# Five small reorderings in a decoder step on one core: a query broadcast moved to another queue, weight splits ahead of key pages, two groups of stores and sums put elsewhere

## The chip, the cores and the metric

The kernel runs on one core of a Trainium2 chip. The metric is the device time of one execution in microseconds (us). Three runs of the kernel before took 1029.35, 1026.24 and 1020.0 us, so the median is 1026.24 us. A core has four compute engines that run their own instruction streams in order: TensorE (PE, matrix products), VectorE (DVE), ScalarE (ACT) and GpSimd (POOL). SyncE (SP) only starts transfers here. ACT and POOL start transfers too.

## What is computed

The reference is one layer of a hybrid decoder for 512 prompt tokens and 8 sample tokens that share all weights (520 columns in all, called NT in the code; they are worked in two halves of 260).

```python
h = rms_norm(x, norm1_g) * (1.0 + sc1) + sh1
z = h @ w_in                       # xr, gr, q, k, v, forget logits, ga, gb
xc, conv_new = causal_dwconv(xr, conv_buf, conv_w, conv_b)
hr, h_last = rg_lru(xc, h0, pos0, rg_wr, rg_br, rg_wi, rg_bi, rg_lambda)
ya = (hr * jax.nn.gelu(gr)) @ w_proj_a
yb = attend(q, k, v, logf).reshape(B, T, ATTN_W) @ w_proj_b   # samples: paged cache of 1024 rows
mixed = (jax.nn.sigmoid(ga) * ya + jax.nn.sigmoid(gb) * yb) @ w_o
x = x + g1 * mixed
h2 = rms_norm(x, norm2_g) * (1.0 + sc2) + sh2
gu, up = jnp.split(h2 @ w_ffn_in, 2, axis=-1)
x = x + g2 * ((jax.nn.silu(gu) * up) @ w_ffn_out)
```

The outputs are the final norm of x, the new keys, values and forget values, the last three inputs of the convolution (convT) and the last state of the recurrence (rgT).

## The kernel before, in words

**Products.** Everything is held transposed, features on the 128 partitions and tokens along the row. Every float32 operand of a large product is split into a high and a low part (for weights `whi` and `wlo`, for h `hh` and `hl`), and a product of one 128-feature weight tile by eight k tiles is 24 matmuls of 260 columns for each half: high by high, low by high, high by low. A weight travels in *chunks* of 256 columns from memory into `wraw` (SP, L210; two buffers), ACT casts the high part (L246), DVE subtracts it to get the low part (L248). A *unit* is one such 128-column weight tile; units are numbered by `state["n"]` in the order in which PE uses them. Unit 0 and 1 are the query tiles q6 and q7, units 2 and 3 are the convolution inputs xr0 and xr1 (one chunk, one `wraw`), unit 4 is the gate tile ga0. `begin()` (L285) opens a unit: it runs `tick()`, then loads chunks ahead, then splits weights ahead (`split_upto`), then issues stores. The list of instructions in each engine is laid down by a scheduler from the order of the code, from dependencies and from explicit ties (`issue_after`), so an edit in the code need not move anything.

**Queries.** The tiles q0 to q5 are made from two partial sums: PE makes the second half and DVE adds the first (L926). `q_done` (L878) stores the query tile, and transposes its sample columns on PE into `qt` (L883), from which the samples' queries go through memory (`qtd`) and come back spread over all partitions as `qb`. `after[0] = after[1]` (L928) ties the low parts of units 0 and 1 behind the add of query tile 2.

**Keys of the cache.** `tick()` multiplies key pages of the samples by the broadcast query (L743, `pg<-pg,qb`) and sums them by head (L744), on DVE. `key_halves` (L707) loads two half pages on POOL and, for the first pages of a sample, issues the broadcast of half a query row (L716), on POOL as well. Its second broadcast (sample 1, first half) stands on POOL behind the running sums of the forget values (`after`, L456).

**Decays.** `decay_load` (L1211) reads rows of forget sums spread over the partitions (`fb<-ftd`, L1214) on SP, for attention over the prompt. The stores of convT and rgT (L1136, L1137) stand ahead of it in the code.

**Join.** The samples' attention over the cache ends in `fold_values` (L849: one product `pvs` on PE, one copy `pvt` on ACT), and `join_values` (L1351) mixes it with the new token's value on DVE (L1355 to L1357) and writes it into the sample columns of the operand of w_proj_b (L1359 on ACT, L1360 on DVE). `join()` runs both in the middle of the first half of the first w_proj_b product, and the second half of that product reads the result. On POOL, L1306 finishes the prompt part of the last tile of that operand.

**Norm 2 and block sums.** `h2_half(1)` (L1484) makes the second half of h2 tile by tile f = 0 to 7: DVE scales x (L1500), POOL finishes the sample columns (L1502, L1503), ACT casts the high part (L1505, L1511), DVE (even f) or ACT (odd f) finishes the float32 value (L1509, L1507), DVE subtracts to get the low part (L1512). PE consumes tile after tile in the first products of the feed-forward layer (L305 `fi`). The rest of that layer uses sums of blocks of h2: `h2_blocks(k)` (L1631) makes four differences on POOL from tiles k and k + 4, for k = 0 to 3, and DVE and ACT split them later (`split_blocks`, L1640).

## Time and profile before

| | us |
|---|---|
| runs shown | 1029.35, 1026.24, 1020.0 (median 1026.24) |
| the profiled execution | 1021.18 |
| its span, first to last instruction | 1019.1 |
| outside the span (1021.18 - 1019.1) | 2.1 |
| PE busy | 994.4 |
| DVE busy | 793.0 |
| ACT busy | 548.2 |
| POOL busy | 329.4 |

The page gives the granted clock of PE as 0.997 of full speed over the span. The timeline view has one row for an instruction or a run of equal ones: its start and its duration in us from the start of the span, engine, source line, operation, the written tile `<-` the read ones, the count after an x, and in brackets the idle time ahead of it with what ended it. PE's matmuls overlap: a row lasts some 0.28 us, but the next one starts 0.12 us after it, so time lost on PE is read from the starts of two rows: their distance less 0.12. SPq is the queue of transfers that SP starts; a DMA row there is the issue, not the transfer. The waits view adds up such idle times by waiting and releasing instruction.

### The profile page before, as it was taken

The numbers are of one execution on the slowest core, as the hardware profiler recorded it, in microseconds if no ns is written. First come the engines' busy times: TensorE is split into PE (matmuls) and PEld (weight loads), VectorE is DVE, ScalarE is ACT, GpSimd is POOL, SyncE is SP. The second block draws the span as 40 slices with busy tenths as digits, with TensorE's granted clock in tenths as the row PEclk, the third lists the DMA queues.
The fourth block names the chain that finished last, engine by engine and source line by source line (L and its number), as shares of the span: only waits on it lengthen the run. The fifth ranks groups of instructions, "written<-read, shape, count | busy, mean of one in ns | idle before, by whom it ended". The sixth has DMA issues, their size and how long they took to land.

```text
span 1019.1 us, 21277 instructions
## 1 busy us (share of the span) xinstructions
PE 994.4 (98%) x8012; PEld 920.4 (90%) x8012; DVE 793.0 (78%) x1423; ACT 548.2 (54%) x1128; POOL 329.4 (32%) x416
## 2 busy tenths in 40 slices
PE   5999999999999999999999999999999999999996
PEld 2799999999998988888888888999999999999996
DVE  5559999998998887887655544868888888888865
ACT  4534476858761576777783233554444444445453
POOL 0347211111134146554500001583342433425112
PEclk9999999999999999999999999999999999999998
DMA  9797857788889999997867996324234243233222
GB/s 325 250 326 261 253 184 196 231 269 271 283 260 331 342 301 280 309 275 242 254 212 265 319 329 196 83 64 125 80 107 123 65 125 87 81 104 104 63 64 84
DMA packets 164313, 206.97 MB, mean 203 GB/s; under 512 B 9826, under 2 KB 125042, under 8 KB 164146
## 3 DMA queue, kind: packets, MB, share of 16 engines
q1 hardware_dynamic: 147490, 152.52, 48.2%
q0 software_dynamic: 13040, 46.67, 13.9%
q10 hardware_dynamic: 3680, 6.42, 1.7%
q8 instruction: 63, 1.03, 0.4%
q14 instruction: 40, 0.33, 0.1%
HBM read 192.49 MB, written 13.09 MB: 202 GB/s over the span
## 4 chain that ended last, share of the span: by engine, by line
PE 89%; DMA 4%; DVE 2%; ACT 1%; issue 1%; POOL 1%; POOLq 0%; SPq 0%; DVEq 0%; ACTq 0%
PE fo L305 12%; PE k L305 5%; PE wo L305 5%; PE gb L305 5%; PE gr L305 5%; PE ga L305 5%; PE pb L305 5%; PE v L305 4%; PE xr L305 4%; PE pv L836 3%; PE pa L305 3%; PE po L1301 2%; PE qp L540 2%; PE ada L372 2%; PE ptt L1267 2%; PE fi L305 1%
## 5 line engine op out<-in xcount | busy, mean ns | idle before, releaser
L246 ACT CAST whi<-wraw 128x1024 fp32r<-128x1024 f32 (+1 forms) x79 | 82.0, 1039 | 110.7 <-PE pb L305 34.3
L248 DVE TENSOR_TENSOR wlo<-wraw,whi 128x1024 fp32r<-128x1024 f32 (+1 forms) x79 | 99.2, 1256 | 21.2 <-ACT whi L246 18.8
L270 ACT CAST wb<-ws 128x512 fp32r<-128x512 f32 x72 | 44.8, 622 | 93.2 <-PE fo L305 64.6
L305 PE MATMUL fo<-ach,wb 128*128 128x260 f32 x512 | 93.5, 282 | 0.0
L698 POOL DMA_DIRECT2D pg<-in_cache_k_dram x74 | 39.6, 536 | 144.9 <-DVE S L748 62.8
L271 DVE TENSOR_TENSOR wb<-wraw,wb 128x512 fp32r<-128x512 f32 x86 | 75.6, 879 | 5.9 <-ACT wb L270 4.7
L305 PEld LDWEIGHTS fo<-ach,wb 128*128 128x128 f32 x512 | 79.1, 188 | 0.0
L271 DVE TENSOR_TENSOR wb<-ws,wb 128x512 fp32r<-128x512 f32 x72 | 64.4, 894 | 14.1 <-ACT wb L270 12.2
L261 POOL TENSOR_TENSOR ws<-wraw 128x512 f32<-128x512 f32 x18 | 24.5, 1361 | 156.9 <-DMA wraw<-in_w_fi_dram 92.0
L305 PE MATMUL fo<-acl,wb 128*128 128x260 f32 x256 | 72.5, 283 | 0.0
L270 ACT CAST wb<-wraw 128x512 fp32r<-128x512 f32 x86 | 53.5, 622 | 33.3 <-ACT cp L1676 6.4
L747 DVE TENSOR_TENSOR pg<-pg,qb 128x1024 f32<-128x1024 f32 x48 | 57.8, 1218 | 3.0 <-DMA pg<-in_cache_k_dram 3.0
L748 DVE TENSOR_REDUCE S<-pg 128x16 f32<-128x1024 f32 x48 | 57.4, 1208 | 0.2
L1258 POOL TENSOR_SCALAR p<-p,mu 128x128 f32<-128x128 f32 (+3 forms) x28 | 38.6, 1391 | 53.1 <-DVE mu L1254 47.2
L305 PEld LDWEIGHTS fo<-acl,wb 128*128 128x128 f32 x256 | 48.1, 188 | 0.0
L1252 ACT ACTIVATE p<-p,mu 128x128 f32<-128x128 f32 (+3 forms) x64 | 35.4, 554 | 18.0 <-DVE mu L1251 17.8
L305 PE MATMUL v<-hh,whi 128*128 128x260 f32 x128 | 37.3, 292 | 0.8 <-ACT row L816 0.5
L305 PE MATMUL pb<-oh,whi 128*128 128x260 f32 x128 | 37.2, 291 | 0.3 <-ACT oh L1359 0.3
L305 PE MATMUL xr<-hh,wlo 128*128 128x260 f32 x128 | 36.3, 283 | 1.1 <-DVE wlo L248 1.1
L305 PE MATMUL k<-hh,whi 128*128 128x260 f32 x128 | 37.3, 291 | 0.0
L305 PE MATMUL gb<-hh,whi 128*128 128x260 f32 x128 | 37.0, 289 | 0.0
L305 PE MATMUL xr<-hh,whi 128*128 128x260 f32 x128 | 36.7, 287 | 0.0
(1101 smaller groups left out, 3957.0 us busy)
## 6 DMA issues: line engine op xcount, KB each, us to landing
araw<-in_ada_w_dram SPq DMA_DIRECT2D x48, 512.0 KB, 7.6
wraw<-in_w_fi_dram SPq DMA_DIRECT2D x44, 512.0 KB, 4.2
pg<-in_cache_k_dram POOLq DMA_DIRECT2D x42, 512.0 KB, 6.3
pg<-in_cache_v_dram SPq DMA_DIRECT2D x42, 512.0 KB, 5.3
wraw<-in_w_in_dram SPq DMA_DIRECT2D x34, 512.0 KB, 7.9
wraw<-in_w_in_dram SPq DMA_DIRECT2D x11, 1024.0 KB, 8.9
pg<-in_cache_v_dram POOLq DMA_DIRECT2D x22, 512.0 KB, 6.4
pg<-in_cache_k_dram POOLq DMA_DIRECT2D x32, 256.0 KB, 5.2
```

The source lines that it names most:

```text
L246: state["act"] = act.copy(hi[:, :k1 - k0], src)
L248: state["last"] = dve.tensor_tensor(lo[:, :k1 - k0], src, hi[:, :k1 - k0].bitcast(F32), ALU.subtract)
L261: pool.tensor_tensor(s1, a21, a22, ALU.add)
L270: state["act"] = act.copy(t[:, :4], src)
L271: state["last"] = dve.tensor_tensor(t[:, 4:], src, t[:, :4].bitcast(F32), ALU.subtract)
L305: state["mm"] = pe.matmul(out[:, :t1 - t0], lhsT=wt[k], rhs=at, start=k == 0 and m == 0, stop=k == nk - 1 and m == 2)
L698: done.append(eng.dma_start(pg, cache[bass.ds(r, 1), :, c0:c1].rearrange("a p c -> (a p) c")))
L747: dve.tensor_tensor(pg, pg, q, ALU.mult)
L748: last = dve.tensor_reduce(S[r // 2][:, c:c + H], pg.rearrange("p (h d) -> p h d", d=DH), AX.X, ALU.add)
L836: pe.matmul(pv[0][32 * gq:32 * gq + 32, :], lhsT=pw[r][:, c:c + 32], rhs=pgs[gq // 2][:, 512 * hf:512 * hf + 512], start=j == 0, stop=j == ...
L1252: act.activation(p[:, :n + 128], p[:, :n + 128], AF.Exp, bias=mu[:, 0:1], scale=-1.0, accum_out=mu[:, 1:2])
L1258: (pool.tensor_scalar(p, p, mu[:, 2:3], None, ALU.mult) if a and i + 1 < KT else act.activation(p, p, AF.Copy, scale=mu[:, 2:3]))
```

## The change

1. *Queries.* The tie of units 0 and 1 moves from the add of query tile 2 to that of tile 3.
2. *Splits ahead of key pages.* When unit 1 opens, the weights are split ahead first, and only then `tick()` runs.
3. *A query broadcast on SP.* While `state["n"]` is 1, `key_halves` issues the query broadcast on SP instead of POOL. That is the one for sample 1, first half.
4. *Decay loads ahead of two stores.* The stores of convT and rgT stand in the code behind the first key product, the query loads and the decay loads.
5. *Join.* `fold_values` runs ahead of the first w_proj_b product instead of inside it, and the two products in `join_values` change places.
6. *Block sums.* The four groups go in the order k = 3, 0, 1, 2; the first instruction is now the one that reads the second halves of tiles 3 and 7, and all others are tied behind it.

```diff
@@ begin
+        if n == 1:
+            split_upto(reach(n, last, state["lead"]))
         if n < 42:
             tick(KEYS[n], n in VALUES)
@@ key_halves
-            pool.dma_start(qb[0], qtd[s:s + 1, 512 * half:512 * half + 512].partition_broadcast(128))
+            eng = sp if state["n"] == 1 else pool
+            eng.dma_start(qb[0], qtd[s:s + 1, 512 * half:512 * half + 512].partition_broadcast(128))
@@ queries
-                if i == 2:
+                if i == 3:
                     after[0] = after[1] = state["qadd"]
@@ behind the recurrence
-    sp.dma_start(convT, conv_out)
-    sp.dma_start(rgT, rg_out)
@@ join_values
+        dve.tensor_tensor(v8v, v8v, xv[:, :, 1], ALU.mult)
         dve.tensor_tensor(o8v, pvv, xv[:, :, 0], ALU.mult)
-        dve.tensor_tensor(v8v, v8v, xv[:, :, 1], ALU.mult)
@@ ahead of the attention
     decay_load(0)
+    sp.dma_start(convT, conv_out)
+    sp.dma_start(rgT, rg_out)
@@ last attention tile
             some_values(32)
+            assert not values_todo and not chains
+            fold_values(*pv.pop("todo"))
@@ join
-        assert not values_todo and not chains
-        fold_values(*pv.pop("todo"))
         join_values()
@@ h2_blocks
-        pool.tensor_tensor(u[:, L_], b1[:, R_], b1[:, L_], ALU.subtract)
-        pool.tensor_tensor(w[:, L_], b2[:, R_], u[:, L_], ALU.subtract)
-        pool.tensor_tensor(w[:, R_], b2[:, R_], b1[:, R_], ALU.subtract)
-        pool.tensor_tensor(u[:, R_], b2[:, L_], w[:, L_], ALU.subtract)
-        traw.append((u, w))
+        with tc.issue_after(state["blocks"].ins) if k != 3 else nullcontext():
+            first = pool.tensor_tensor(w[:, R_], b2[:, R_], b1[:, R_], ALU.subtract)
+        if k == 3:
+            state["blocks"] = first
+        with tc.issue_after(state["blocks"].ins):
+            pool.tensor_tensor(u[:, L_], b1[:, R_], b1[:, L_], ALU.subtract)
+            pool.tensor_tensor(w[:, L_], b2[:, R_], u[:, L_], ALU.subtract)
+            pool.tensor_tensor(u[:, R_], b2[:, L_], w[:, L_], ALU.subtract)
+        traw[k] = u, w
@@ feed-forward
-            for k in range(4):
+            for k in (3, 0, 1, 2):
                 h2_blocks(k)
```

The built programs show what moved. The first place is DVE while PE makes the query tiles q3 and q4 (`q3_0` is the first half of tile 3, `wlo_711` and `wlo_756` are units 0 and 1). Before:

```order
L926 TENSOR_TENSOR qp_109<-q2_1_659,qp_109 128x260
L248 TENSOR_TENSOR wlo_711<-wraw_565,whi_710 128x1024
L926 TENSOR_TENSOR qp_110<-q3_0_679,qp_110 128x260
L926 TENSOR_TENSOR qp_110<-q3_1_693,qp_110 128x260
L248 TENSOR_TENSOR wlo_756<-wraw_565,whi_755 128x1024
L926 TENSOR_TENSOR qp_111<-q4_0_723,qp_111 128x260
```

On DVE at the same place, now:

```order
L929 TENSOR_TENSOR qp_109<-q2_1_659,qp_109 128x260
L929 TENSOR_TENSOR qp_110<-q3_0_679,qp_110 128x260
L929 TENSOR_TENSOR qp_110<-q3_1_693,qp_110 128x260
L248 TENSOR_TENSOR wlo_711<-wraw_565,whi_710 128x1024
L248 TENSOR_TENSOR wlo_756<-wraw_565,whi_755 128x1024
L929 TENSOR_TENSOR qp_111<-q4_0_723,qp_111 128x260
```

Both low parts now stand behind the two adds of query tile 3; the first one stood ahead of them.

The second place is DVE ahead of xr1 (`wlo_1063` is unit 2, `wlo_1186` unit 3, `wlo_1258` unit 4, `qb_1037` the broadcast that goes to SP, `gws` splits of the recurrence's gate weights). Before:

```order
L248 TENSOR_TENSOR wlo_1063<-wraw_759,whi_1062 128x1024
L914 TENSOR_TENSOR gws_1121<-gw_917,gws_1121 128x256
L914 TENSOR_TENSOR gws_1124<-gw_917,gws_1124 128x256
L743 TENSOR_TENSOR pg_1016<-pg_1016,qb_1037 128x1024
L743 TENSOR_TENSOR pg_1039<-pg_1039,qb_1037 128x1024
L744 TENSOR_REDUCE S_761<-pg_1016 128x2x8
L744 TENSOR_REDUCE S_761<-pg_1039 128x2x8
L248 TENSOR_TENSOR wlo_1186<-wraw_759,whi_1185 128x1024
L743 TENSOR_TENSOR pg_1143<-pg_1143,qb_1037 128x1024
```

On DVE there, now (unit 3 is `wlo_1140`):

```order
L917 TENSOR_TENSOR gws_1124<-gw_917,gws_1124 128x256
L248 TENSOR_TENSOR wlo_1140<-wraw_759,whi_1139 128x1024
L746 TENSOR_TENSOR pg_1016<-pg_1016,qb_1037 128x1024
L746 TENSOR_TENSOR pg_1039<-pg_1039,qb_1037 128x1024
L747 TENSOR_REDUCE S_761<-pg_1016 128x2x8
L747 TENSOR_REDUCE S_761<-pg_1039 128x2x8
L746 TENSOR_TENSOR pg_1147<-pg_1147,qb_1037 128x1024
L746 TENSOR_TENSOR pg_1168<-pg_1168,qb_1037 128x1024
L747 TENSOR_REDUCE S_761<-pg_1147 128x2x8
L747 TENSOR_REDUCE S_761<-pg_1168 128x2x8
L248 TENSOR_TENSOR wlo_1258<-wraw_1060,whi_1257 128x1024
```

The low part of unit 3 went ahead of the first four key instructions; unit 4 still stands behind all eight. On SP the new broadcast stands between the chunk of unit 4 and the store of query tile 6, and the next chunk's load stands ahead of the store of query tile 7 instead of behind it.

The third place is POOL behind norm 2 (`h2r_9373`, `9386`, `9399`, `9412` hold tiles 0 and 1, 2 and 3, 4 and 5, 6 and 7). Before:

```order
L1503 TENSOR_TENSOR h2r_9412<-h2r_9412,mod_102 128x2x8
L1634 TENSOR_TENSOR u_9961<-h2r_9373 128x260
L1636 TENSOR_TENSOR w_9962<-h2r_9399,h2r_9373 128x260
L1635 TENSOR_TENSOR w_9962<-h2r_9399,u_9961 128x260
L1634 TENSOR_TENSOR u_9967<-h2r_9373 128x260
L1637 TENSOR_TENSOR u_9961<-h2r_9399,w_9962 128x260
```

On POOL at the same place, now (`u_9961` and `w_9962` are those of k = 3):

```order
L1506 TENSOR_TENSOR h2r_9412<-h2r_9412,mod_102 128x2x8
L1638 TENSOR_TENSOR w_9962<-h2r_9412,h2r_9386 128x260
L1642 TENSOR_TENSOR u_9961<-h2r_9386 128x260
L1638 TENSOR_TENSOR w_9968<-h2r_9399,h2r_9373 128x260
L1643 TENSOR_TENSOR w_9962<-h2r_9412,u_9961 128x260
L1642 TENSOR_TENSOR u_9967<-h2r_9373 128x260
```

The first block sum now reads tiles 3 and 7, so all sixteen stand behind the last tile of norm 2; they began with tiles 0 and 4.

Of the rest: on PE `pvs` (one product) stands directly behind `xp` and ahead of the first w_proj_b matmul, where twelve of that product's matmuls stood ahead of it. On SP the order around edit 4 is the same in both programs: the stores of rgT and convT, the loads qA and qB, then the loads `fb`. The number of matmuls, splits and transfers is the same.

More of the change, by code (lines that the diff above doesn't have):

```diff
@@ L1628 @@
     L_, R_ = slice(0, HALF), slice(HALF, NT)
-    tb, traw = [], []
+    tb, traw = [], {}
     def h2_blocks(k):
```

## The prediction

> **What bounds the kernel now.** I read the page's busy times first, then the waits of PE alone, then the timeline around each of those waits on the engines that end it.
>
> ```profile
> PE 994.4 (98%) x8012; PEld 920.4 (90%) x8012; DVE 793.0 (78%) x1423; ACT 548.2 (54%) x1128; POOL 329.4 (32%) x416
> ...
> PE fi L305 <- DVE h2l L1512: 1.1, 2, 0.8
> PE xr L305 <- DVE wlo L248: 1.1, 1, 1.1
> PE qt L883 <- DVE qp L926: 0.8, 1, 0.8
> PE pv L836 <- DMA pg<-in_cache_v_dram: 0.4, 1, 0.4
> ...
> PE pb L305 <- ACT oh L1359: 0.3, 1, 0.3
> ```
>
> PE is busy 98% of the span, and no matmul is removed, so the only thing to win is idle time of PE. The waits name five stops that the edits touch: the feed-forward start (1.1), xr1 (1.1), the query transposes (0.8), the value pages (0.4), the join (0.3), 3.7 us together. Behind each of them PE goes on without a long idle stretch, so a stop that goes moves all that follows, and the end with it. Nothing here can be worth 1% (10 us); the danger is only that something new makes PE wait.
>
> **Edit 1, query transposes.** Timeline of PE, then of DVE:
>
> ```profile
> 61.89 0.28 PE L540 MATMUL q<-hl,whi 128*128 128x260 f32 x1
> ...
> 62.48 0.29 PE L540 MATMUL q<-hh,whi 128*128 128x260 f32 x1
> 63.59 0.27 PE L883 MATMUL qt<-cs,qp 128*8 128x128 f32 x1 [0.83 <-DVE qp L926]
> ...
> 61.64 1.23 DVE L248 TENSOR_TENSOR wlo<-wraw,whi 128x1024 fp32r<-128x1024 f32 x1 [2.00 <-ACT whi L246]
> 62.78 0.76 DVE L926 TENSOR_TENSOR qp<-q,qp 128x260 f32<-128x260 f32 x2
> ```
>
> The transposes of tile 3 start 1.11 us behind the matmul ahead of them, 0.99 more than the 0.12 step. The tile's last matmul ends at 62.17, but DVE is in unit 0's low part until 62.87 and both adds (0.76) come after it. With the low parts behind, the second add runs at about 62.2, ends at about 62.6, and PE, there at 62.6, hardly waits. Upper end 0.99, lower end 0.36 (if the second add only starts as PE arrives, 62.76 plus half of 0.76 and a signal); I take 0.85, near the row. The two low parts end about 0.2 later; the chunk load that waits for their buffer goes 0.2 later, and its low part stands behind key sums on DVE anyway (row 85.63 below). Cost 0.
>
> **Edits 2 and 3, xr1.** PE, then DVE, then POOL, SP and the moved bytes of the window 60 to 100 us (40 slices of 1 us), then two rows of the transfers:
>
> ```profile
> 93.70 0.37 PE L305 MATMUL xr<-hh,whi 128*128 128x260 f32 x1
> 95.12 0.40 PE L305 MATMUL xr<-hh,wlo 128*128 128x260 f32 x1 [1.05 <-DVE wlo L248]
> ...
> 100.99 0.28 PE L305 MATMUL ga<-hh,wlo 128*128 128x260 f32 x1
> ...
> 85.63 1.42 DVE L248 TENSOR_TENSOR wlo<-wraw,whi 128x1024 fp32r<-128x1024 f32 x1
> 86.97 0.97 DVE L914 TENSOR_TENSOR gws<-gw,gws 128x256 fp32r<-128x256 f32 x2
> 89.31 2.36 DVE L743 TENSOR_TENSOR pg<-pg,qb 128x1024 f32<-128x1024 f32 x2 [1.37 <-DMA qb<-qtd]
> ...
> 93.84 1.22 DVE L248 TENSOR_TENSOR wlo<-wraw,whi 128x1024 fp32r<-128x1024 f32 x1
> ...
> 99.50 1.22 DVE L248 TENSOR_TENSOR wlo<-wraw,whi 128x1024 fp32r<-128x1024 f32 x1
> ...
> 69.41 0.54 POOL L716 DMA_DIRECT2D qb<-qtd  x1 [1.41 <-DMA qtd<-qt]
> ...
> 84.95 0.55 POOL L716 DMA_DIRECT2D qb<-qtd  x1
> ...
> 74.98 0.38 SPq L210 DMA_DIRECT2D wraw<-in_w_in_dram  x1
> ...
> GB/s 410 214 220 229 344 394 392 381 380 359 384 379 352 393 390 385 393 378 349 323 188 12 273 252 297 2 168 126 104 352 148 270 421 398 356 213 182 273 310 334
> ...
> gw<-in_gates_dram SPq DMA_DIRECT2D x4, 256.0 KB, 10.4
> ...
> qb<-qtd POOLq DMA_DIRECT2D x4, 256.0 KB, 5.1
> ```
>
> PE loses 95.12 - 93.70 - 0.12 = 1.30 us for unit 3's low part, which DVE reaches at 93.84, behind key sums that had waited 1.37 us for the broadcast. Now it follows the gate splits at 87.94 and is ready at about 89.1, before PE asks for it. The next stop is unit 4. PE asks for its low part at 100.99 - 0.85 - 1.30 = 98.84. On DVE all eight key instructions now stand ahead of it: 99.50 - 89.31 - 1.22 = 8.97 us from 89.1, to 98.1, and 1.22 more makes 99.3. But this DVE chain hangs on the first broadcast, which POOL issues when `qtd` is stored (row 69.41, 1.41 of waiting), and that store follows the transposes of edit 1: 0.85 earlier gives 98.5, ready by 0.3. So the gain is 1.30, or 0.8 if the first broadcast does not come earlier; I take 1.2, nearer the case in which the chain of stores holds.
>
> That needs the broadcast on SP to land by 89.1 - 0.85 = 88.2. SP issues it behind the chunk at 74.98, at 75.4; its query has been in memory since before 69.41, so SP does not stand still on it, and the store of query tile 6 behind it is not held. The row of POOL's broadcasts (5.1) puts the landing at 80.5; the slowest row of equal size on SP (10.4) at 85.8. The bytes speak for the early end: in this window the engines run near 380 GB/s until 80 and are down to 12 GB/s at 81, so a further 256 KB is through a microsecond later. POOL is rid of one issue of 0.55. The next chunk's load goes out 5 to 6 us earlier, when unit 3's low part is done; the store of tile 7 that it passes is read only much later. Both cost 0.
>
> **Edit 4, stores.** The order of SP's instructions did not change there, so the fb loads come when they came. Gain 0; if they did come earlier, at most the 0.4 of the value pages.
>
> **Edit 5, join.** PE, then DVE, then POOL:
>
> ```profile
> 541.35 0.38 PE L305 MATMUL pb<-ol,whi 128*128 128x260 f32 x1
> 542.06 0.39 PE L305 MATMUL pb<-oh,whi 128*128 128x260 f32 x1 [0.32 <-ACT oh L1359]
> ...
> 540.35 1.03 DVE L1355 TENSOR_TENSOR o<-pvt,xw 128x64 f32<-128x64 f32 x1 [0.48 <-ACT pvt L852]
> ...
> 540.01 1.28 POOL L1306 TENSOR_TENSOR ol<-ol,side 128x512 fp32r<-128x512 f32 x1 [19.20 <-DVE ol L1305]
> ```
>
> PE loses 542.06 - 541.35 - 0.12 = 0.59. `pvs` goes 12 matmuls (1.4 us) earlier, at no cost: its input is ready and it is the same one product. DVE then has both products of the join ready at about 539.9, where POOL's L1306 starts too, and that is the matter: the small product took 1.03 us while POOL ran. If POOL holds it again until 541.3, the result is only some 0.17 earlier; if DVE gets both through first, POOL's tile, which PE's matmul of 541.35 reads, is late by their 0.2 to 0.4. Ends 0 and 0.59; I take 0.2, near the row with the two engines side by side.
>
> **Edit 6, block sums.** PE, then DVE, POOL and ACT:
>
> ```profile
> 665.61 0.28 PE L305 MATMUL fi<-h2h,wlo 128*128 128x260 f32 x1
> 666.72 0.39 PE L305 MATMUL fi<-h2l,whi 128*128 128x260 f32 x1 [0.82 <-DVE h2l L1512]
> ...
> 667.60 0.39 PE L305 MATMUL fi<-h2l,whi 128*128 128x260 f32 x1 [0.24 <-DVE h2l L1512]
> ...
> 668.65 0.40 PE L305 MATMUL fi<-h2l,whi 128*128 128x260 f32 x2
> ...
> 664.07 0.78 DVE L1512 TENSOR_TENSOR h2l<-h2r,h2h 128x260 fp32r<-128x260 f32 x2
> ...
> 665.70 1.84 DVE L1512 TENSOR_TENSOR h2l<-h2r,h2h 128x260 fp32r<-128x260 f32 x2
> ...
> 667.80 0.63 DVE L1512 TENSOR_TENSOR h2l<-h2r,h2h 128x260 fp32r<-128x260 f32 x1
> ...
> 665.60 0.78 POOL L1636 TENSOR_TENSOR w<-h2r 128x260 f32<-128x260 f32 x1
> ...
> 664.85 0.58 ACT L1507 ACTIVATE h2r<-h2r,mod,n2amp 128x252 f32<-128x252 f32 x1
> ...
> 666.29 0.58 ACT L1507 ACTIVATE h2r<-h2r,mod,n2amp 128x252 f32<-128x252 f32 x1
> ```
>
> Two low parts take 0.78 us without block sums beside them and 1.84 with. PE stands for tile 5 (666.72 - 665.61 - 0.12 = 0.99) and tile 6 (0.41 by the same reading), 1.40 in all. Without POOL, tile 5's low part starts when ACT is done (664.85 + 0.58 = 665.43), takes 0.4 and lets PE go at about 665.95, so 0.22 of the 0.99 stays; tile 6 is ready in time; 1.18 is gained. But POOL's first sum now starts at 666.9, when ACT ends tile 7 (666.29 + 0.58), and tile 7's low part on DVE waits for the same event. PE wants that one 1.05 behind tile 6 (668.65 - 667.60), now at 667.41. If DVE goes first it is ready at 667.4; if POOL goes first (0.78), at 668.1, and 0.74 of the gain is lost. Ends 0.44 and 1.18; I take 0.8. The sums end some 2 us later, and what reads them is split several microseconds after that beside a PE that needs it later still; cost 0.
>
> [...]
>
> **The sum.** 0.85 + 1.2 + 0 + 0.2 + 0.8 = 3.05 us; ends 0.36 + 0.8 + 0 + 0.44 = 1.6 and 0.99 + 1.30 + 0.59 + 1.18 = 4.1. The profiled execution would go from 1021.18 to 1018.1. That execution is 5.1 below the median of the runs shown (1026.24), which lie between 1020.0 and 1029.35; the mean of all four is 1024.2, and 3.05 off that is 1021.1, which I predict.
>
> **Rivals.**
> *POOL goes first* at both places where it meets DVE: 0.85 + 1.2 + 0.17 + 0.44 = 2.7, so 1021.5. For it: POOL and DVE start on the same event. Against it: in the trace DVE starts sooner behind a signal.
> *The stop moves to unit 4, slower than before.* If SP serves the broadcast only behind the whole chunk, both as slow as the slow row, it lands at 75.4 + 2 x 10.4 = 96.2. DVE stands 8.0 us, with unit 4 behind it, and PE with it: 3.05 less 8.0 is a loss of 5.0, so 1029.2. It decides from a landing at about 91.3. Against it: the queues are empty at 81.
> *Edit 4 does bring the loads earlier*: 0.4 more, 1020.7. Against it: the order of SP.
> *No stop is really shortened*, because PE meets another late input within the same stretch each time: 1024.2. For it: at unit 4 the margin is 0.3 us.
>
> **How the numbers follow.** My forecast 0.63, POOL first 0.20, the stop at unit 4 0.05, edit 4 at work 0.04, no stop shortened 0.08. The spread between runs is wider than the difference of all but one case: the range goes from 1020.0 - 4.1 = 1015.9 to 1029.35 - 1.6 = 1027.8. About 1% is what a measurement of this kernel can tell from no change. No case reaches 10 us, so faster by over 1% (0.05) and slower by over 1% (0.03) are left to the spread of the runs and to a mechanism that I do not see; within 1% has 0.92.
>
> **What would show it.** In PE's waits: `qt` for `qp` gone or below 0.2; `xr` for `wlo` gone and no `ga` for `wlo`; `fi` for `h2l` at 0.2 to 0.9 instead of 1.1; `pb` for `oh` at 0.3 or less; `pv` for the value pages as before. On SP the broadcast at about 75, on DVE no wait for `qb` near 89. Wrong would be a `ga` that waits, a `pb` that waits for POOL by more than 0.5, or a span longer than 1019.1.

## The result, and the profile after

The changed kernel takes 1018.5 us in the median of 22 runs (1015.94 to 1023.24), the kernel before 1022.72 us in the median of 22 runs on the same chips (1017.86 to 1030.0). The ratio is 0.9961 with a 95% interval from 0.9943 to 0.9979: about 4 us less (2 to 6), within 1%. The profiled execution took 1017.75 us where that of before took 1021.18; its span is 1016.0 us (before 1019.1).

The busy times of the page, then PE's waits in the changed kernel. Lines are shifted: L307 is the former L305, L929 the former L926, L1515 the former L1512, and the others move likewise by 1 to 3.

```profile
PE 992.3 (98%) x8012; PEld 920.1 (91%) x8012; DVE 797.9 (79%) x1423; ACT 547.1 (54%) x1128; POOL 324.4 (32%) x415
```

```profile
PE pa L307 <- DVE wlo L248: 0.7, 1, 0.7
...
PE xr L307 <- DVE wlo L248: 0.5, 1, 0.5
...
PE pb L307 <- ACT oh L1360: 0.2, 1, 0.2
```

The rows of `qt` (0.8) and `fi` (1.1) are gone, `xr` fell from 1.1 to 0.5, `pb` from 0.3 to 0.2. But this `xr` is another one: it is unit 2 (xr0), which did not stop before, and not unit 3 (xr1). The row of `pa` is new and stands in no other trace; the last section comes back to it. The timeline of that stretch in the changed kernel, by engines (PE, ACT, POOL, SP, DVE):

```profile
62.82 0.29 PE L542 MATMUL q<-hh,whi 128*128 128x260 f32 x1
63.03 0.27 PE L886 MATMUL qt<-cs,qp 128*8 128x128 f32 x1
...
87.25 0.37 PE L307 MATMUL xr<-hh,whi 128*128 128x260 f32 x1
88.11 0.39 PE L307 MATMUL xr<-hh,wlo 128*128 128x260 f32 x1 [0.49 <-DVE wlo L248]
...
99.74 0.28 PE L307 MATMUL ga<-hh,whi 128*128 128x260 f32 x1
100.10 0.39 PE L307 MATMUL ga<-hh,wlo 128*128 128x260 f32 x1
...
62.65 2.00 ACT L246 CAST whi<-wraw 128x1024 fp32r<-128x1024 f32 x2 [9.39 <-DMA wraw<-in_w_in_dram]
64.56 0.58 ACT L892 ACTIVATE qt<-qt 8x512 f32<-8x512 f32 x1
...
70.38 0.54 POOL L719 DMA_DIRECT2D qb<-qtd  x1 [3.07 <-DMA qtd<-qt]
...
74.89 1.43 SPq L719 DMA_DIRECT2D qb<-qtd  x1
...
77.06 2.49 DVE L746 TENSOR_TENSOR pg<-pg,qb 128x1024 f32<-128x1024 f32 x2 [3.73 <-DMA qb<-qtd]
...
86.60 1.46 DVE L248 TENSOR_TENSOR wlo<-wraw,whi 128x1024 fp32r<-128x1024 f32 x1
...
89.78 2.35 DVE L746 TENSOR_TENSOR pg<-pg,qb 128x1024 f32<-128x1024 f32 x2
```

At 63.03 the transposes start without a stop. At 74.89 the second broadcast goes out on SP, and at 89.78 DVE no longer waits for `qb`. Between them stands something new. Chunk 0 landed late (ACT's first cast at 62.65; it was at 60.55 before). ACT copies the transposed sample queries (`qt`, 64.56) only behind both casts, so POOL sends the first broadcast at 70.38, later than the 69.41 of before and not earlier. The key sums on DVE end later, unit 2's low part with them (86.60), and PE loses 88.11 - 87.25 - 0.12 = 0.74 us. At `ga` it loses 100.10 - 99.74 - 0.12 = 0.24.

The join and norm 2 in the changed kernel (PE, DVE, POOL):

```profile
539.26 0.38 PE L307 MATMUL pb<-ol,whi 128*128 128x260 f32 x1
539.83 0.39 PE L307 MATMUL pb<-oh,whi 128*128 128x260 f32 x1 [0.19 <-ACT oh L1360]
...
663.36 0.28 PE L307 MATMUL fi<-h2h,wlo 128*128 128x260 f32 x1
663.70 0.38 PE L307 MATMUL fi<-h2l,whi 128*128 128x260 f32 x1
...
537.95 1.34 DVE L1357 TENSOR_TENSOR o<-pvt,xw 128x64 f32<-128x64 f32 x1
...
664.66 0.43 DVE L1515 TENSOR_TENSOR h2l<-h2r,h2h 128x260 fp32r<-128x260 f32 x1
...
537.92 1.29 POOL L1307 TENSOR_TENSOR ol<-ol,side 128x512 fp32r<-128x512 f32 x1 [19.17 <-DVE ol L1306]
...
664.76 0.93 POOL L1638 TENSOR_TENSOR w<-h2r 128x260 f32<-128x260 f32 x1 [2.09 <-issue]
```

In the join POOL went first by 0.03 us, and DVE's small product lasted until POOL was done: 0.45 of the stop of 0.59 is left. At norm 2 DVE went first by 0.10 us, and of 1.40 us of stops 0.22 is left (663.70 - 663.36 - 0.12).

### The profile page after: what moved, and what is told of

The parts are those of the page before. It is cut to its first block, busy times and chain, and to the rows that moved or that the text cites. A ratio compares the mean times of both kernels' runs of the same rounds, so it can differ in the third digit from the quotient of the medians.

```text
span 1016.0 us, 21278 instructions
## 1 busy us (share of the span) xinstructions
PE 992.3 (98%) x8012; PEld 920.1 (91%) x8012; DVE 797.9 (79%) x1423; ACT 547.1 (54%) x1128; POOL 324.4 (32%) x415
## 3 DMA queue, kind: packets, MB, share of 16 engines
q8 instruction: 63, 1.03, 0.4%
## 4 chain that ended last, share of the span: by engine, by line
PE 83%; DVE 8%; DMA 4%; ACT 3%; issue 2%; SPq 0%; DVEq 0%; ACTq 0%; POOLq 0%
PE fo L307 12%; PE wo L307 5%; PE gb L307 5%; PE pb L307 4%; PE ga L307 4%; PE k L307 4%; PE v L307 4%; PE gr L307 3%; PE xr L307 3%; PE pa L307 3%; PE pv L839 3%; PE po L1302 2%; DMA wraw<-in_w_in_dram 2%; PE qp L542 2%; PE ada L374 2%
## 5 line engine op out<-in xcount | busy, mean ns | idle before, releaser
L307 PE MATMUL fo<-ach,wb 128*128 128x260 f32 x512 | 93.4, 283 | 0.0
L307 PEld LDWEIGHTS fo<-ach,wb 128*128 128x128 f32 x512 | 78.9, 188 | 0.0
L307 PE MATMUL fo<-acl,wb 128*128 128x260 f32 x256 | 72.2, 282 | 0.0
L307 PEld LDWEIGHTS fo<-acl,wb 128*128 128x128 f32 x256 | 48.3, 189 | 0.0
L307 PE MATMUL v<-hh,whi 128*128 128x260 f32 x128 | 37.2, 291 | 0.8 <-ACT row L819 0.5
L307 PE MATMUL pb<-oh,whi 128*128 128x260 f32 x128 | 37.1, 290 | 0.2 <-ACT oh L1360 0.2
L307 PE MATMUL k<-hh,whi 128*128 128x260 f32 x128 | 37.3, 291 | 0.0
L307 PE MATMUL gb<-hh,whi 128*128 128x260 f32 x128 | 37.1, 290 | 0.0
L307 PE MATMUL pa<-gh,wlo 128*128 128x260 f32 x128 | 36.2, 284 | 0.7 <-DVE wlo L248 0.7
L307 PE MATMUL xr<-hh,wlo 128*128 128x260 f32 x128 | 36.3, 284 | 0.5 <-DVE wlo L248 0.5
```

Source lines behind the costliest of these rows:

```text
L307: state["mm"] = pe.matmul(out[:, :t1 - t0], lhsT=wt[k], rhs=at, start=k == 0 and m == 0, stop=k == nk - 1 and m == 2)
```

## The experiments

### Both kernels once more

Unchanged kernels, for a second trace each.

> The kernel before once more, unchanged, for a second trace. Theory A (each stop on PE is made by the program's order): the same stops at the same places, within 0.2 us each: the query transposes 1.0, xr1 1.3, the join 0.6, norm 2 1.4 us; xr0 (unit 2) without a stop. Theory B (the stops hang on how transfers land in one execution): at least one of the four differs by over 0.5 us from the first trace. At the value pages (matmuls of pv) and at the start a difference of up to 1 us is expected under both, since they wait for transfers.

Measured: 1020.51 us, span 1018.8. The stops are where they were: transposes 1.13, xr1 1.34, join 0.58, norm 2 0.99 and 0.42, xr0 none. ACT and PE of this run:

```profile
60.77 1.05 ACT L246 CAST whi<-wraw 128x1024 fp32r<-128x1024 f32 x1 [7.76 <-DMA wraw<-in_w_in_dram]
...
63.80 0.27 PE L883 MATMUL qt<-cs,qp 128*8 128x128 f32 x1 [0.96 <-DVE qp L926]
```

> The changed kernel once more, unchanged. In its first trace xr0 stopped for 0.74 us, which it did not in the kernel before, and chunk 0 (units 0 and 1) had landed 2 us later. Theory A: the stop at xr0 comes from that late landing; with ACT's first cast of unit 0 near 60.5 us it is below 0.2. Theory B: it comes from the changed order of the splits and is 0.5 to 0.9 again, whenever chunk 0 lands. Under both: transposes below 0.2, xr1 below 0.2, join 0.4 to 0.5, norm 2 0.2 to 0.3.

Measured: 1017.69 us, span 1016.0. Now no stop at xr0. ACT and DVE of this run:

```profile
62.17 2.01 ACT L246 CAST whi<-wraw 128x1024 fp32r<-128x1024 f32 x2 [8.50 <-DMA wraw<-in_w_in_dram]
64.07 0.58 ACT L892 ACTIVATE qt<-qt 8x512 f32<-8x512 f32 x1
...
86.04 1.36 DVE L248 TENSOR_TENSOR wlo<-wraw,whi 128x1024 fp32r<-128x1024 f32 x1
```

A cast half a microsecond earlier (62.17 instead of 62.65) was enough, together with a PE that came to xr0 0.4 later (87.66 instead of 87.25). So in this order the stop at xr0 hangs on the landing of chunk 0, which differs from execution to execution. Split by starts of PE's groups, the four traces read:

| us | before | again | after | again |
|---|---|---|---|---|
| first query product to `ga` (edits 1 to 3) | 75.32 | 75.57 | 73.55 | 73.37 |
| `ga` to `pb` (no edit on PE but `pvs`, 0.24 later in the code before) | 437.39 | 436.85 | 436.67 | 437.00 |
| `pb` to the feed-forward tile group `fig` (edits 5 and 6) | 138.53 | 138.48 | 136.98 | 137.01 |
| `fig` to the end of PE's last matmul | 333.85 | 333.85 | 333.73 | 333.74 |

The first stretch gives 2.0 us, the third 1.5, of which 0.24 is only `pvs` on the other side of the mark. The second differs by 0.5 between two runs of one kernel. The four stretches add up to 985.1 and 984.8 us before and 980.9 and 981.1 after, 3.9 less; the spans differ by less, since the first query product happened to start later in the two traces of the change (26.19 and 26.03, against 25.55 twice).

### Edits 1 and 6 alone

```diff
-                if i == 2:
+                if i == 3:
                     after[0] = after[1] = state["qadd"]
...
-            for k in range(4):
+            for k in (3, 0, 1, 2):
                 h2_blocks(k)
```

(and `h2_blocks` as in the change)

> Edits 1 and 6 alone, on the kernel before. Theory A (each edit shortens its own stop, and all behind it moves): PE is 0.85 to 0.99 earlier behind the query transposes, keeps the stop of 1.3 at xr1 and the 0.6 of the join, and wins another 1.1 to 1.2 at norm 2, 2.0 in all. If edit 1 makes the stop at xr0, it is there too (0.5 to 0.9); if late landing or edits 2 and 3 make it, it is not. Rival (the gain of edit 1 is only put off to the next stop): the stop at xr1 grows from 1.3 to 2.1 and 1.2 is left in all.

Measured: 1019.47 us, span 1017.7. Chunk 0 came later still (the load went out at 52.94 and took 10.2 us, so it is this landing that the cast waited for, and not the PE product that its row names):

```profile
63.20 2.00 ACT L246 CAST whi<-wraw 128x1024 fp32r<-128x1024 f32 x2 [9.33 <-PE q L540]
...
88.70 0.39 PE L305 MATMUL xr<-hh,wlo 128*128 128x260 f32 x1 [0.48 <-DVE wlo L248]
...
96.07 0.39 PE L305 MATMUL xr<-hh,wlo 128*128 128x260 f32 x1 [1.23 <-DVE wlo L248]
```

No stop at the transposes, but 0.72 at xr0 and 1.48 at xr1, 2.20 together: about the rival's 2.1, at two places and not at one. Against the first trace of before, edit 1 kept 0.1 in this execution: 0.99 less 0.72 less 1.48 - 1.30. Norm 2 has 0.22 left, so edit 6 alone gives its 1.2, and the stop at xr0 needs neither edit 2 nor edit 3.

### Edits 2, 3 and 5 alone

```diff
+        if n == 1:
+            split_upto(reach(n, last, state["lead"]))
...
+            eng = sp if state["n"] == 1 else pool
+            eng.dma_start(qb[0], qtd[s:s + 1, 512 * half:512 * half + 512].partition_broadcast(128))
...
+            fold_values(*pv.pop("todo"))
```

(edits 2, 3 and 5 of the change, whole)

> Edits 2, 3 and 5 alone, on the kernel before. Theory A: the stop of 1.0 at the query transposes stays, that at xr1 (1.3) goes, ga waits below 0.3, the join keeps 0.4 to 0.5 of its 0.6, norm 2 keeps 1.4: 1.4 to 1.7 in all. If edit 2 or 3 makes the stop at xr0 in the changed kernel, it is there (0.5 to 0.9). Rival for the join (the gain there comes from the earlier product on PE, not from the exchange on DVE, and the product that meets POOL's tile still takes over 1 us): DVE's product of the samples' attention takes 1.2 to 1.4 us and ends within 0.1 of POOL's tile.

Measured: 1028.02 us, span 1026.3, which no theory expected. ACT, then PE:

```profile
68.14 1.99 ACT L246 CAST whi<-wraw 128x1024 fp32r<-128x1024 f32 x2 [14.68 <-DMA wraw<-in_w_in_dram]
...
71.17 0.38 PE L886 MATMUL qt<-cs,qp 128*8 128x128 f32 x1 [7.86 <-DVE qp L929]
```

The load of chunk 0 went out at 52.54, as ever, and took 15.5 us (8.5 in the first trace of before). Without edit 1, the adds of query tile 3 stand behind unit 0's low part on DVE, and PE stood for 8.03 us. No stop at xr0, xr1 or `ga`, but with PE this late that says nothing on edits 2 and 3. The join kept 0.44, with DVE's product at 1.34 us and done 0.07 behind POOL's tile, as the rival for the join had it.

This gave the theory that the next runs test: *chunk 0's landing varies, and edit 1 decides what a late one costs.* With casts at 60.55, 60.77 and 68.14 the transposes started at 63.59, 63.80 and 71.17: 3.04, 3.03 and 3.03 later.

### Chunk 0 loaded late on purpose, without and with edit 1

In the kernel before and in the changed one the same edit:

```diff
-    load_chunks(0)
     sp.dma_start(cs[:, C_TRI:], cst[:, C_TRI:])
...
-        sp.dma_start(qd[i], t)
+        st = sp.dma_start(qd[i], t)
+        state.setdefault("q0", st)
...
         if i == 3:
+            with tc.issue_after(state["q0"].ins):
+                load_chunks(0)
             split_upto(0)
```

> The kernel before, with the load of chunk 0 (units 0 and 1) tied behind the store of query tile 0, so that it goes out some 2.7 us later (55.4 instead of 52.7). In six traces so far the cast of unit 0 began at 60.55 to 68.14 us, and PE's stop at the query transposes in the old order was 0.99, 1.13 and 8.03 for casts at 60.55, 60.77 and 68.14. Theory A (chunk 0's landing sets the stop, microsecond for microsecond, from a cast at about 59.7 on): a stop of 3.0 to 4.5 at the transposes and a median 2 to 3.5 us above the kernel before. Rival (the landing varies but PE has work to put ahead of it): stop and median as before, within 1 us.

Measured: 1030.28 us (1029.24 to 1031.32, 4 runs), ratio to the kernel before 1.0077 (1.0052 to 1.0103). The load, issued at 55.35, took until 68.6, and PE stood for 8.05 us:

```profile
68.63 1.99 ACT L246 CAST whi<-wraw 128x1024 fp32r<-128x1024 f32 x2 [15.16 <-DMA wraw<-in_w_in_dram]
...
71.33 0.37 PE L883 MATMUL qt<-cs,qp 128*8 128x128 f32 x1 [7.89 <-DVE qp L926]
```

> The same late chunk in the changed kernel. Theory A1 (edit 1 takes chunk 0 out of the way altogether, until query tile 6 uses it near 69 us): no stop at the transposes nor at xr0 above 0.8, median within 1 us of the changed kernel. Theory A2 (edit 1 only moves the deadline by some 2.5 us: ACT casts both units ahead of the samples' queries, which then go out late, come back late on DVE, and hold unit 2's low part behind the key sums): no stop at the transposes, but one of 2.5 to 4 at xr0, median 2 to 3 us above the changed kernel.

Measured: 1022.99 us (1019.62 to 1028.54, 10 runs), ratio to the kernel before 1.0014 (0.9995 to 1.0034); cast at 69.28. That is 4.5 above the changed kernel with an early chunk. The stop at the transposes of tile 3 is gone; xr0 stops for 91.81 - 90.05 - 0.12 = 1.64:

```profile
90.05 0.37 PE L307 MATMUL xr<-hh,whi 128*128 128x260 f32 x1
91.81 0.39 PE L307 MATMUL xr<-hh,wlo 128*128 128x260 f32 x1 [1.40 <-DVE wlo L248]
```

So theory A holds for the order before in its direction (stop and median rose by more than its 3.0 to 4.5 and 2 to 3.5, since the load was slow as well as late), and A2 for the changed one: edit 1 moves the deadline and does not remove it. A2's sizes are off too: the stop at xr0 is smaller than its 2.5 to 4, the median further up than its 2 to 3. In this trace the clock of PE fell as well (last section). The two intervals are apart: with a late chunk the change is worth 7.3 us.

### The queries' copy ahead of the casts

On the changed kernel; ACT's copy and store of `qt` now stand ahead of the casts of units 0 and 1:

```diff
-            split_upto(0)
+            load_chunks(0)
             gate_load(0)
...
+            with tc.issue_after(state["qt"].ins):
                 split_upto(1)
...
         if i == 3:
             q_done(*ready.pop())
+            with tc.issue_after(state["qt"].ins):
+                split_upto(0)
```

(`state["qt"]` is the store of `qt`)

> The changed kernel with ACT's copy and store of the transposed sample queries ahead of the casts of units 0 and 1 (tie only, chunk 0 loaded as ever). Theory A2: the copy starts right behind the transposes (63.5 to 64.2 us) whenever chunk 0 lands, xr0 never stops (below 0.2), and the median lies 0 to 1 us below the changed kernel, since only executions with a late chunk gain. Rival (the casts then come too late for query tile 6, or the chunk of units 2 and 3 too late for xr0): a stop at query tile 6 or at xr0 of 0.5 or more.

Measured: 1017.85 us (1016.65 to 1021.43, 5 runs), ratio 0.9952 (0.9925 to 0.998). The copy runs at 62.47, and xr0 has no stop:

```profile
62.47 0.59 ACT L892 ACTIVATE qt<-qt 8x512 f32<-8x512 f32 x1 [10.08 <-PE qt L886]
```

The same with chunk 0 loaded late, by the edit of the section above:

> Both: the queries' copy and store ahead of the casts, and chunk 0 loaded 2.7 us later. Theory A2: the late chunk costs nothing here: no stop above 0.3 at the transposes, query tile 6 and xr0, median within 1 us of the kernel with the copy first and an early chunk, and 2 or more below the changed kernel with the late chunk. Theory A1 or another cause of the stop at xr0: the same loss as in the changed kernel with the late chunk.

Measured: 1020.79 us (1017.87 to 1025.64), ratio 0.9978 (0.9957 to 0.9999). It is 2.2 below the changed kernel with the late chunk, but 2.9 above this section's first kernel: the late chunk still costs, where A2 had expected nothing. xr0 stops for 1.48, by another road. DVE in this run, the fastest of its ten:

```profile
69.70 2.36 DVE L248 TENSOR_TENSOR wlo<-wraw,whi 128x1024 fp32r<-128x1024 f32 x2 [3.76 <-ACT whi L246]
...
77.11 1.22 DVE L745 TENSOR_TENSOR pg<-pg,qb 128x1024 f32<-128x1024 f32 x1
```

The broadcast is there in time (no wait for `qb` at 77.11; in the kernel with the early chunk the keys began at 74.85), but DVE itself had stood 3.76 us for chunk 0's casts, with the decay constants and then the key pages behind it. A2 named one of two ways in which a late chunk reaches xr0.

### Edit 3 alone, and block sums as a train

On the kernel before: the broadcast on SP, and the block sums as in the change but with the four that read only tiles 0 to 3 ahead of all others.

```diff
+            eng = sp if state["n"] == 1 else pool
...
+            for k in range(4):
+                h2_first(k)
+            for k in (3, 0, 1, 2):
                 h2_blocks(k)
```

(`h2_first` makes `u[:, L_]` alone, `h2_blocks` the other three)

> Two places far apart, on the kernel before. First, edit 3 alone (broadcast on SP, no split ahead). Theory A (the 1.37 us that DVE stands for the broadcast are the whole stop at xr1, so edit 3 needs no edit 2): the stop at xr1 falls from 1.3 to below 0.3, ga does not wait. Rival (the split ahead of the key pages is what does it): 0.9 or more stays. Second, block sums in the changed order but with the four that read only tiles 0 to 3 put ahead, as one train of four POOL instructions of some 0.72 us right behind norm 2's last small products. Theory L (DVE is kept out while POOL works through a train, as in the changed kernel at 309.42, where two small DVE instructions took 4.38 us beside a POOL train of 3.67): DVE's low parts of tiles 5 to 7 wait for the end of the train and PE loses 2.0 to 3.3 in all (1.40 in the kernel before, 0.22 in the changed one). Theory S (each low part only runs longer beside POOL, 0.92 instead of 0.39): PE loses 0.4 to 1.3.

Measured: 1024.19 us, span 1022.5. Cast at 64.25, transposes at 67.29, a stop of 3.45; with PE so late, xr1 did not stop, and the first question has no answer here. The second has one (DVE, then POOL):

```profile
668.69 1.69 DVE L1513 TENSOR_TENSOR h2l<-h2r,h2h 128x260 fp32r<-128x260 f32 x2
...
668.38 3.50 POOL L1635 TENSOR_TENSOR u<-h2r 128x260 f32<-128x260 f32 x4
```

DVE's two low parts, issued in the middle of POOL's train, were through after 1.69 us and not at its end (671.88). PE lost 0.61 + 0.43 = 1.04, within theory S and half of the least that L allows. Each of the two took 0.81 or 0.96 and ended 0.3 us behind the end of a POOL instruction, as if the engines took turns.

### Edit 2 alone, and the join without POOL

On the kernel before, edits 2 and 5, and POOL's instruction ahead of the join cut into two halves on DVE:

```diff
-        pool.tensor_tensor(ol[:, :NP], ol[:, :NP].bitcast(F32), side, ALU.add)
+        if i < KT - 1:
+            pool.tensor_tensor(ol[:, :NP], ol[:, :NP].bitcast(F32), side, ALU.add)
...
+            if i == KT - 1 and a == 0:
+                dve.tensor_tensor(ol[pr, :NP], ol[pr, :NP].bitcast(F32), side[pr], ALU.add)
...
         dve.tensor_tensor(o8, o8, v8, ALU.add)
+        dve.tensor_tensor(ol[pr, :NP], ol[pr, :NP].bitcast(F32), side[pr], ALU.add)
```

> Again two places, on the kernel before. First, edit 2 alone (split ahead, broadcast still on POOL at about 85). Theory A2 (the split ahead alone also does it, since unit 4 has 0.1 to 0.3 to spare behind eight key instructions that start at 89.3): xr1 below 0.2, ga below 0.4. Rival (without the early broadcast the stop moves to ga): ga 0.8 or more. Second, edit 5 with POOL's last instruction ahead of the join (L1306, 1.28 us) given to DVE in two halves of 64 partitions, the first in a gap of 0.5, the second behind the join's product. Theory L (POOL's instruction holds the join's product: 1.34 us where it takes 0.2 alone): the product takes 0.2 to 0.4 and PE's stop at the join falls from 0.45 to 0 to 0.2. Rival (the product waits for something else, or DVE's two halves take its place): the product stays near 1 us, or PE waits 0.3 or more for either input. The scheduler also puts three small products of the modulation and three loads elsewhere behind the join.

Measured: 1028.45 us, span 1026.3, with a cast at 66.73 and a stop of 6.83 at the transposes: again no answer on edit 2. The join on DVE:

```profile
547.07 0.22 DVE L1363 TENSOR_TENSOR o<-pvt,xw 128x64 f32<-128x64 f32 x1
547.32 0.69 DVE L1367 TENSOR_TENSOR ol<-ol,side 64x512 fp32r<-64x512 f32 x1
```

The product that took 1.03 and 1.34 us beside POOL takes 0.22 without it. PE's stop at the join fell to 0.24 and not to 0, since the second half now stands ahead of the sum.

### All of it together

The kernel with the copy first and the join on DVE (the two edits above).

> The changed kernel with the queries' copy first (as in the run before) and the last part of the join on DVE. If gains add up: 0 to 1 us below the changed kernel for the copy and 0.3 to 0.45 for the join, so a median of 1017 to 1018 where the kernel before has 1022.7, and a ratio of 0.994 to 0.996. Rival (the join's gain is taken back later, as PE waits for something else within the half): no better than the kernel with the copy first alone, 1017.9 or more.

Measured: 1018.98 us (1018.19 to 1021.57), ratio 0.9964 (0.9944 to 0.9984): no better than the change itself. PE around the join:

```profile
539.81 1.06 PE L374 MATMUL ada<-araw,silc 128*32 128x512 f32 x6
540.80 0.39 PE L307 MATMUL pb<-ol,whi 128*128 128x260 f32 x1
...
543.62 1.90 PE L374 MATMUL ada<-araw,silc 128*32 128x512 f32 x10
```

The scheduler moved small products of the modulation (`ada`): six of the sixteen that stand together in the changed kernel (one row of 1.92 us at 542.88 there) now stand apart, and they take 1.06 us while the other ten still take 1.90. From `pb` to `fig` this kernel takes 137.67 us where the changed kernel takes 136.98. The rival was right.

### The change without edit 1

```diff
-                if i == 3:
+                if i == 2:
                     after[0] = after[1] = state["qadd"]
```

> The changed kernel without edit 1: the low parts of units 0 and 1 stand again ahead of the adds of query tile 3. Theory B (chunk 0 lands at 60.5 to 63 us in most executions and later in some, and without edit 1 PE's stop at the transposes follows the landing from 59.6 on): the median is 1.5 to 3 us above the changed kernel's 1018.5, more than the 0.85 forecast, and the slowest runs are 4 or more above. Theory A (edit 1 is worth what one trace showed, 0.9): 1019.0 to 1019.6. Its own trace should show a stop at the transposes of (cast of unit 0 - 59.6) and xr1 without one.

Measured: 1021.01 us (1018.39 to 1025.84), ratio 0.9981 (0.9956 to 1.0006). That is 2 us more by the ratios, in theory B's range, but the intervals overlap, so the times alone do not decide. The trace shows which mechanism is at work, in one execution:

```profile
61.91 1.99 ACT L246 CAST whi<-wraw 128x1024 fp32r<-128x1024 f32 x2 [8.94 <-DMA wraw<-in_w_in_dram]
...
64.94 0.27 PE L886 MATMUL qt<-cs,qp 128*8 128x128 f32 x1 [2.13 <-DVE qp L929]
```

A stop of 2.30 us (61.91 - 59.6 = 2.31 was expected), and none at xr0, xr1 or `ga`. All executions without edit 1 in one table:

| cast of unit 0 | transposes start | difference | stop on PE | span |
|---|---|---|---|---|
| 60.55 (before) | 63.59 | 3.04 | 0.99 | 1019.1 |
| 60.77 (before again) | 63.80 | 3.03 | 1.13 | 1018.8 |
| 61.91 (without edit 1) | 64.94 | 3.03 | 2.30 | 1018.3 |
| 64.25 (edit 3, train) | 67.29 | 3.04 | 3.45 | 1022.5 |
| 66.73 (edits 2 and 5, join) | 69.76 | 3.03 | 6.83 | 1026.3 |
| 68.14 (edits 2, 3, 5) | 71.17 | 3.03 | 8.03 | 1026.3 |
| 68.63 (before, late chunk) | 71.33 | 2.70 | 8.05 | 1027.2 |

In the first six the difference is a constant of the order on DVE: cast, low part, two adds. In the last, the edit also changed that order: one of the two adds (61.32) had run ahead of the low part, and 0.33 us is missing.

## Why the prediction came out as it did

The direction and the small size were right, and the profiled execution landed where the sum put it (1017.75 for 1018.1). That close a hit is luck in part: in that execution the stops that the sum names shrank by 0.25 (edit 1, with xr0 set against it), 1.06 (edits 2 and 3, with `ga`), 0.14 and 1.18, 2.6 together, and the rest came from stretches that no edit was counted for. The median came out at 1018.5 where 1021.1 was predicted: 1.5 of that is the base (1024.2 from four executions, 1022.72 in 22), the rest a gain of about 4 instead of 3.05, which the interval of 2 to 6 does not tell apart. By its steps:

- **Edit 1** (0.85, ends 0.36 and 0.99). The stop went, all of it. The size was wrong in two ways. The cost of 0 failed, and with it the step of the next item that the first broadcast goes out 0.85 earlier: it went at 70.38 and 69.83 instead of 69.41, because ACT has two casts ahead of the copy of `qt`, which I had not read. And the stop itself is no constant: I took it from one trace, whose load of chunk 0 took 8.5 us, the shortest of the eleven traces in which that load was not moved (8.5 to 15.5, the middle one 10.2). At the cast of the changed kernel's own trace, 62.65, the order before would have started the transposes at 65.68 by the table's constant instead of 63.03; with 0.74 given back at xr0 that leaves 1.9, and 1.8 at the second trace's 62.17, twice what was forecast. These two are worked out, not run.
- **Edits 2 and 3** (1.2, 0.8 to 1.30). xr1's stop of 1.30 and 1.34 is gone in both traces of the change and in the one without edit 1, and DVE's wait for `qb` with it. `ga` waits 0.24 in one trace and 0.15 in the other, and 0.23 or 0.24 in all three later kernels with the copy first and in the one with the late chunk: the margin of 0.3 was not there, and by the prediction's own sign, a `ga` that waits, this step was a little off. Which of the two edits does it stays open: both trials fell on a late chunk. In the kernel before with the late chunk there is no stop at xr1 either, so with a late chunk these edits are worth little.
- **Edit 4** (0). It was not run alone; the order on SP around it is the same in both programs. The stop at the value pages went in the first trace of the change and is back in the second (0.4), and the stretch from `ga` to `pb` differs by 0.5 us between two runs of the kernel before: this is the spread of such pages.
- **Join** (0.2, 0 to 0.59). 0.14, and for the reason given for the low end: POOL first, product held. All seven traces with edit 5 and POOL in its place show this (0.44 or 0.45 left, product 1.34 or 1.35).
- **Norm 2** (0.8, 0.44 to 1.18). 1.18, the end in which DVE goes first; the middle that I took did not occur. In all eight traces with edit 6, 0.21 to 0.26 is left. Without edit 6 the stops there came to 1.02 to 1.43 in five traces, so most of the gain is there each time. At both places whoever came first, by 0.03 us in the join and 0.10 here, ran its normal time or near it, and the other took longer: in the join POOL 1.29 us (1.28 before) and DVE's product 1.34 (0.22 without POOL), here DVE's low part 0.43 (0.39 without block sums) and POOL's sum 0.93 (0.74 each for the next two). (The last section has a row that does not fit.) So the rival *POOL goes first* came true at one of its two places.

In the traces the stages give 2.0 + 0.14 + 1.2 us, so 3.05 was about right for executions like the profiled one. For what the median may have gained beyond that, the runs show a late chunk, for which edit 1 is worth more: the eleven landings go from 60.5 to 68.0, the middle one is at 63.1, the profiled one was the earliest. It also fits what the prediction only noted, that the profiled execution lay 5.1 us below the median of the runs shown. The granted clocks of the executions that were not profiled point the same way. The three traces with stops of 6.8 to 8.1 us at the transposes have a mean clock of 0.991 or 0.992. Of 44 executions of the kernel before that were measured beside the experiments, 15 have 0.994 or less, and all 15 took over 1024 us; of the twelve without edit 1, four, its four slowest; of the 22 of the change, none. Where the clock fell in those executions was not seen. How much of the 4 us a late chunk carries, the times do not settle either: the ratios with and without edit 1 have intervals that overlap, and a second thing differs between executions, a fall of the clock in the attention, at 463 to 475 us, that costs 1.5 us (last section). The rival *no stop really shortened* came true in a single execution, for edit 1 alone, at a cast of 63.20.

## What to carry to other kernels

The stop behind chunk 0 had no one size: in the eleven traces that load took 8.5 to 15.5 us, and in the six of them without edit 1 PE stood 0.99 to 8.03 us behind it. So before costing a stop that ends on a transfer, compare the wait's duration with the spread between runs, and ask how late that transfer comes in the executions that were not profiled. An edit that takes a late transfer out of an engine's in-order stream can be worth more than the one trace shows, as edit 1 was with the late chunk (a stop of 8.05 us without it, one of 1.64 with it), but follow every instruction still queued behind it on each engine (here ACT's casts, then DVE's low parts), because the next of them sets the new deadline. When two engines start on the same event and one may hold the other, as DVE's product was here (1.34 us beside POOL, 0.22 without), take the two ends as cases; the mean of them did not occur at either place here.

## What the runs showed of the hardware

*Equal loads, unequal times.* Transfers of chunk 0 in the kernel before and in the one with edits 2, 3 and 5 (queue, count, KB, us from issue to landing):

```profile
wraw<-in_w_in_dram SPq DMA_DIRECT2D x1, 1024.0 KB, 8.5
```

```profile
wraw<-in_w_in_dram SPq DMA_DIRECT2D x1, 1024.0 KB, 15.5
```

Issued between 51.5 and 53.2 us in all of the eleven traces, the same megabyte took 8.5 to 15.5 us. What decides it was not tried.

*With the stops of 3.45 us and more PE's granted clock was about halved (0.50 to 0.62 over 4 us in the three traces read).* Columns: stretch, PE busy time and matmuls, the like for PEld, DVE, ACT and POOL, granted clock, DMA share, GB/s. Behind the stop of 3.45 us, then behind the stop of 2.30 us:

```profile
66.00:70.00 4.00, 2.71 (x13) 2.72 (x14) 2.79 (x5) 1.98 (x4) 1.90 (x3) 0.52 0.84 294
70.00:74.00 4.00, 4.00 (x24) 3.63 (x23) 1.93 (x18) 0.45 (x2) 1.84 (x5) 0.62 1.01 340
```

```profile
66.00:70.00 4.00, 4.00 (x36) 3.77 (x35) 2.77 (x21) 1.96 (x4) 1.68 (x4) 1.00 1.01 334
```

PE issued 36 matmuls in 4 us at a clock of 1.00, and 24 at 0.62. So the stop of 3.45 us was paid for twice and the one of 2.30 was not: from PE's first product into `q` to `ga` these two runs take 54.3 and 50.6 us, 3.7 apart for stops 1.15 apart. The clock fell with the three longer stops at the transposes too (0.50 from 70 to 74 us in the traces with 8.03 and 8.05 us, a mean of 0.992 over the whole span in the one with 6.83), which makes a late chunk dearer still in the order before. In the trace with 3.45 us the fall began before the stop ended: from 66.0 to 66.5 us the clock was already 0.68, when PE had stood for under 2.7 us, and the next matmul came at 67.29. The length of the stop alone does not explain the fall, as a third row shows. In the changed kernel with the late chunk the longest stop ahead was 0.61 us, followed by sixteen small transposes of 64 columns, and the clock still fell:

```profile
76.00:80.00 4.00, 4.00 (x23) 4.00 (x22) 3.59 (x20) 1.52 (x3) 1.07 (x2) 0.57 1.04 361
```

Four other traces (before again, the kernel before with the late chunk, edit 2 with the join on DVE, the change without edit 1) have such a fall in the attention as well, with no stop of PE over 0.55 us near it. In the second trace of before the clock was 0.50 from 464 to 466 us, and the products of one value tile took 4.51 us from 462.64 (as long from 462.94 in the change without edit 1), where the changed kernel takes 2.98: 1.5 us that the first trace of before does not pay. These are four of the seven traces without edit 1, and none of the seven with it has the fall; what brings it about was not tried.

*One DVE instruction held through a whole train.* In the first trace of the changed kernel a DVE sum of 128 elements, which takes 0.39 us alone, lasted 4.07 us beside nine POOL instructions between 309.86 and 313.53. DVE came late to what stood behind it, the low part that PE waited 0.96 us for at 319.04 (the row of `pa`). In nine of the other traces the sum had run before POOL came and took 0.38 or 0.39, in one 0.41; in three POOL's first instruction came 0.26 to 0.34 us behind it, and it took 0.60. Here POOL came 0.14 us behind it, so who comes first does not explain it. In the train made on purpose the engines took turns. What makes the difference was not settled.

```profile
309.72 4.07 DVE L788 TENSOR_TENSOR S<-S,suf 128x128 f32<-128x128 f32 x1
```
